# Attention with its value tiles loaded from DRAM: the loads issued from ScalarE's queue in place of SyncE's

## The chip, the core and the metric

The kernel runs on one core of a Trainium2 chip. A core has five engines with an instruction queue each: TensorE (PE: matrix products and transposes into PSUM; its weight loads, PEld, are listed on their own), VectorE (DVE), ScalarE (ACT), GpSimd (POOL) and SyncE (SP, which only issues DMAs and waits). An instruction in a queue waits for semaphores that other engines' instructions or DMAs raise, and what stands behind it in the same queue waits with it. A DMA can be issued from SP's queue or from ACT's (SPq and ACTq in the profile); its data are moved by 16 DMA engines that all queues share.

The metric is the device time of one execution in microseconds (us), and of several executions the median.

## The reference

One decoder layer on 1024 positions of 1024 channels, all in float32. The normalised input is projected; a quarter of the channels goes through a pooling mixer, three quarters through attention with 12 heads of 64. Every head is evaluated with three patterns (all keys of the last 128, every 4th of the last 512, every 16th of the last 2048), and the three results are merged by their softmax denominators. Then come the output projection and a gated feed-forward block. Cut to what matters here:

```python
q, k, v = ...                                  # (B, S, 12, 64) each, of the projection
q, k = rope(q, pos), rope(k, pos)
for window, dilation in ((128, 1), (512, 4), (2048, 16)):
    o, lse = dilated_branch(q, k, v, window, dilation)   # softmax(q k^T / 8, masked) v
    outs.append(o); lses.append(lse)
w = softmax(stack(lses), axis=0)
attn_out = sum(w[..., None] * stack(outs), axis=0)
mix = concatenate([pool_out, attn_out], axis=-1) @ w_out
x = x + rms_norm(mix)
f = (silu(h @ w_gate) * (h @ w_up)) @ w_down             # h = rms_norm(x)
x = x + rms_norm(f)
```

## The kernel before

**Heads and units.** The 12 heads are worked on in six pairs (`pr.p` from 0 to 5). Each pair has two units: `h` = 0 for the first 512 positions, where one dense score table with counted masks serves all three patterns (`dense`), and `h` = 1 for the last 512, with two tables: side 0 for the near keys, side 1 for the keys of the same class modulo 4 (`scores`). So there are 12 units; those of pairs 0 to 3 follow each other, then come (4, 0), (5, 0), (4, 1), (5, 1).

**The stages of a unit.** PE makes the scores into a bank `ps_s`. VectorE adds the mask and takes the extreme (L761, L827), ACT exponentiates in place (L764, L830). For `h` = 1 the two tables are merged (`others`, L853; `join`, L866 to L883), and the rows are weighted on POOL, VectorE or ACT (`weigh`, L894 to L914). PE transposes the weighted rows into `ps_t` (`turn`), ACT copies the high part of the result into `ptr` (L965), VectorE the remainder (L966), and PE multiplies `ptr` with the values into `ps_o` (`product`). At the end of a head ACT and VectorE take `ps_o` out (L1009, L1010) and make the high and low parts of the mix (L924 to L928), which SP stores (L931). Between these steps PE's program has the next pairs' projections (`ps_pj`), whose weights SP loads (L329, L332) and ACT and POOL or VectorE split into high and low parts (L336, L340), and whose results are rotated by VectorE and POOL with the tables `cosr` and `sinr` (L529 to L534). Every float32 product is made of three products of such high and low parts.

**The values.** They are projected for two pairs at once (`v_rows`, and `rows_first` for the first two pairs), split into high and low parts, and stored by SP in the DRAM tensor `vd`, with the positions as rows (L679, L1079). From there each pair's values come back in four loads of 512 KB: `v_load`, L709. Two of them hold the rows in their natural grouping (`nat` = 0: four blocks of 128 positions), two the rows by class modulo 4 (`nat` = 1), for each half `h`. The first of the four is due at one point of the plan, the other three together at another; the table `vt` has the two points of each pair, counted in units.

**Where they go.** `room` picks the place. Pairs 0 to 4 share four tiles of the pool `att` with one buffer each; for `h` = 0 the tags change places from pair to pair, so that the first load of a pair goes into the tile that the former pair is done with first. A load therefore waits for PE's last product with the former pair's values in that tile, as well as for the landing of the stores in `vd`. Pair 5 puts its two loads of `h` = 0 into the places of the tables `cosr` and `sinr`, which must have been read by the last rotation, and the other two into `vlast`.

**What sets the order.** The points at which every step is written into the program are a plan by hand, in units (`put`, `emit`). PE's instructions keep the program's order (`keep_in_program_order`). The order of the others on VectorE, ACT, POOL and SP is worked out when the program is built: a planner runs the program on a model of the chip's times and takes, on each queue, what is ready and of highest priority; some groups have a raised priority (`high_priority`). A DMA is an item of the queue from which it is issued, and it is planned there. The semaphores are added after that.

In the program before, ACT's queue issues three DMAs at the start and two at the end; all others, the 24 loads of L709 among them, are in SP's queue.

Of the kernel before, what the change touches and what calls it, by code (L numbers as in the profile page):

```python
# [8 lines left out]
F32 = mybir.dt.float32  # L9
# [277 lines left out]
def hybrid_block(ctx: ExitStack, tc: tile.TileContext, xT, w_in, w_v, w_vp, w_pool, w_out, w_gate, w_up, w_down,  # L287
                 g1, g2, g3, g4, pscale, cost, sint, maskA, maskB, maskD, quadA, quadB, lsel, ident, perm, band, out):
    nc = tc.nc
# [85 lines left out]
    def slot(k, shape, dt, name):  # L375

        return xgp.tile(shape, dt, name=name, tag="xk%d" % k)
# [190 lines left out]
    def did(key):  # L568
        seen[key] = seen.get(key, 0) + 1

    def need(key, n):
        assert seen.get(key, 0) >= n, (key, n, seen.get(key, 0))
# [116 lines left out]
    def v_load(pr):  # L689

        pr.v = {}

        def room(nat, h):
            if pr.p < NPAIR - 1:
                return att.tile([P, 4, 2, 2, 64], F32R, name="v%d" % nat, tag="v%d%d" % (nat if h else (nat + pr.p) % 2, h),
                                bufs=1)
            if h == 0:

                return att.tile([P, 4, 2, 2, 64], F32R, name="v%d" % nat, tag=("cosr", "sinr")[nat], bufs=1)
            if "v" not in pr.st:  # L700
                pr.st["v"] = slot(4, [P, 2, 4, 2, 2, 64], F32R, "vlast")
            return pr.st["v"][:, nat]

        def load(*which):
            for nat, h in which:
                need(("vd", pr.p // 2, h), 2)
                src = vd[pr.p // 2, h * 512:h * 512 + 512, pr.p % 2 * 256:pr.p % 2 * 256 + 256]
                pr.v[nat, h] = room(nat, h)
                nc.sync.dma_start(pr.v[nat, h].bitcast(F32).rearrange("p b a n f -> p b (a n f)"),  # L709
                                  src.rearrange("(j r) f -> r j f", j=4) if nat == 0 else  # L710
                                  src.rearrange("(r c) f -> r c f", c=4))
                did(("t", pr.p))
            due["v", pr.p, h] = clock[0] + 4.0
        return [lambda: load((0, 0)), lambda: load((1, 0), (1, 1), (0, 1))]
# [431 lines left out]
    for p in range(NPAIR):  # L1146
        pr = Pair()
# [74 lines left out]
    for p in range(1, 4):  # L1222
        pr = pairs[p]
# [824 lines left out]
```

## Time and profile before

| | us |
|---|---|
| median of 3 runs | 1109.18 |
| lowest and highest of them | 1108.96, 1109.7 |
| the profiled execution | 1111.03 |
| its span, first to last instruction | 1109.2 |

| engine | busy us | share of the span |
|---|---|---|
| PE | 1094.4 | 99% |
| VectorE | 782.9 | 71% |
| ACT | 550.7 | 50% |
| POOL | 529.7 | 48% |

The granted clock of TensorE was 0.997 of the full one on the mean.

All rows are of this one execution; times of day are counted from the start of its span. A row of the timeline has the start, the duration, the engine (with a q for its queue: a DMA issue or a wait), the line, the operation and the tiles, written out of the tile left of the arrow; in brackets stands the idle time of the engine before it and what ended it. A row of waits has who waited, for whom, the total in us, the number of times and the longest. The chain of work that ended last goes back from the last instruction, at each step to what released it. Matrix products overlap, so that a PE that is shown busy may still have lost a tenth of a microsecond here and there.

### The profile page before, as it was taken

To read this page: it belongs to the slowest core of one execution; us is meant where nothing else is said; L and a number is where in the kernel's file an instruction comes from. 1 tells how busy PE (TensorE), PEld (TensorE's weight loads), DVE (VectorE), ACT (ScalarE), POOL (GpSimd) and SP (SyncE) were. 2 spreads that over 40 slices of the span, in tenths; PEclk is the share of its full clock that TensorE was granted. 3 is DMA by queue.
4 is the path that set the end of the run, shared out by engine and by line. 5 is a ranking of instruction groups with operands and counts; after the bars stand their busy time and mean duration, and the time that the engine had idled before them with its cause. 6 is when DMAs were issued, how large, how long until landed. Compare 5 with 4: busy or idle time off the path is not lost.

```text
span 1109.2 us, 16017 instructions
## 1 busy us (share of the span) xinstructions
PE 1094.4 (99%) x5646; PEld 929.6 (84%) x5646; DVE 782.9 (71%) x1356; ACT 550.7 (50%) x985; POOL 529.7 (48%) x425
## 2 busy tenths in 40 slices
PE   9999999999999999999999999999999999999997
PEld 7888899989888888888887888888888888888886
DVE  7967978787978758799777777667566462343674
ACT  7456767676777755866222222233222544343432
POOL 0111617263554021100666777686568896666521
PEclk9999999999999999999999999999999999999998
DMA  8225232424149448654466666543445896656442
GB/s 294 95 75 190 96 134 73 156 72 176 58 154 336 156 144 307 225 218 161 164 225 237 237 237 228 209 170 123 152 179 213 277 353 202 206 180 203 133 152 77
DMA packets 91296, 201.81 MB, mean 182 GB/s; under 512 B 9296, under 2 KB 25168, under 8 KB 89808
## 3 DMA queue, kind: packets, MB, share of 16 engines
q1 hardware_dynamic: 90240, 200.00, 51.4%
q8 instruction: 44, 0.72, 0.3%
q10 hardware_dynamic: 976, 0.79, 0.2%
q14 instruction: 36, 0.29, 0.1%
HBM read 143.87 MB, written 56.89 MB: 181 GB/s over the span
## 4 chain that ended last, share of the span: by engine, by line
PE 88%; DVE 5%; ACT 2%; DMA 2%; POOL 2%; issue 1%; ACTq 0%; DVEq 0%; POOLq 0%
PE ps_pj L292 26%; PE ps_s L292 25%; PE ps_o L292 24%; PE ps_t L292 10%; PE ps_t L295 2%; DMA bd<-sq 1%; POOL whl L340 1%; DMA v<-vd 1%; DVE pp L912 1%; DVE ptr L966 0%; DVE ql L561 0%; ACT ptr L965 0%; DMA wraw<-in_w_in_dram 0%; DVE rsw L529 0%; DVE qh L560 0%
## 5 line engine op out<-in xcount | busy, mean ns | idle before, releaser
L292 PE MATMUL ps_o<-tT,fw 128*128 128x512 f32 x648 | 151.0, 390 | 0.8 <-DVE sq L1665 0.8
L292 PEld LDWEIGHTS ps_o<-tT,fw 128*128 128x128 f32 x648 | 121.3, 188 | 26.9 <-issue 1.6
L292 PE MATMUL ps_pj<-x,whl 128*128 128x512 f32 x480 | 131.5, 399 | 0.2 <-DVE whl L340 0.2
L1482 POOL TENSOR_TENSOR fw<-rw,fw 128x512 fp32r<-128x512 f32 x72 | 100.2, 1415 | 29.8 <-ACT fw L1480 28.4
L292 PEld LDWEIGHTS ps_pj<-x,whl 128*128 128x128 f32 x480 | 86.4, 188 | 14.6 <-DVE whl L340 0.7
L340 POOL TENSOR_TENSOR whl<-wraw,whl 128x512 fp32r<-128x512 f32 x44 | 60.2, 1390 | 66.9 <-ACT whl L336 62.2
L1777 POOL TENSOR_TENSOR op<-rw,op 128x512 fp32r<-128x512 f32 x38 | 62.2, 1636 | 31.8 <-ACT op L1776 31.8
L366 POOL TENSOR_TENSOR nrr<-nrr,half 128x4 f32<-128x4 f32 (+1 forms) x7 | 6.9, 985 | 141.2 <-ACT eps L365 99.0
L292 PE MATMUL ps_s<-b,fw 128*128 128x512 f32 x312 | 72.5, 389 | 0.0
L1482 POOL TENSOR_TENSOR whl<-rw,whl 128x512 fp32r<-128x512 f32 x30 | 47.8, 1615 | 44.8 <-ACT whl L1480 29.3
L292 PEld LDWEIGHTS ps_s<-b,fw 128*128 128x128 f32 x312 | 58.6, 188 | 12.2
L1776 ACT ACTIVATE op<-rw 128x1024 fp32r<-128x1024 f32 x38 | 40.0, 1059 | 56.4 <-PE ps_t L292 26.5
L1480 ACT ACTIVATE fw<-rw 128x1024 fp32r<-128x1024 f32 x45 | 47.5, 1062 | 37.1 <-PE ps_o L292 15.2
L292 PE MATMUL ps_pj<-whl,x 128*128 128x256 f32 (+1 forms) x432 | 64.7, 298 | 0.0
L966 DVE TENSOR_TENSOR ptr<-ps_t,ptr 128x512 fp32r<-128x512 f32 (+1 forms) x84 | 53.0, 647 | 15.6 <-ACT ptr L965 15.1
L965 ACT ACTIVATE ptr<-ps_t 128x512 fp32r<-128x512 f32 (+1 forms) x84 | 45.2, 561 | 34.0 <-PE ps_t L295 24.7
L292 PEld LDWEIGHTS ps_pj<-whl,x 128*128 128x128 f32 x432 | 57.3, 191 | 2.2
L1778 DVE TENSOR_TENSOR op<-rw,op 128x512 fp32r<-128x512 f32 x33 | 28.9, 875 | 40.7 <-ACT op L1776 33.0
L1777 POOL TENSOR_TENSOR fw<-rw,fw 128x512 fp32r<-128x512 f32 x26 | 42.7, 1641 | 22.5 <-ACT fw L1776 21.0
L830 ACT ACTIVATE pp<-pp,sx 128x256 f32<-128x256 f32 x96 | 47.9, 501 | 8.2 <-DVE sx L827 7.7
L292 PE MATMUL ps_o<-ptr,v 128*128 128x128 f32 (+3 forms) x376 | 50.4, 268 | 1.2 <-DVE ptr L966 0.8
L1480 ACT ACTIVATE whl<-rw 128x1024 fp32r<-128x1024 f32 x19 | 20.2, 1063 | 61.2 <-DVE rw L1595 36.9
(337 smaller groups left out, 2804.2 us busy)
## 6 DMA issues: line engine op xcount, KB each, us to landing
rw<-bd SPq DMA_DIRECT2D x77, 256.0 KB, 4.0
rw<-in_w_gate_dram SPq DMA_DIRECT2D x28, 512.0 KB, 4.5
rw<-in_w_up_dram SPq DMA_DIRECT2D x28, 512.0 KB, 5.8
v<-vd SPq DMA_DIRECT2D x22, 512.0 KB, 5.0
rw<-wsd SPq DMA_DIRECT2D x44, 256.0 KB, 3.8
bd<-p SPq DMA_DIRECT2D x39, 256.0 KB, 2.8
rw<-in_w_down_dram SPq DMA_DIRECT2D x33, 256.0 KB, 4.4
wraw<-in_w_out_dram SPq DMA_DIRECT2D x15, 512.0 KB, 5.5
```

Source lines behind the costliest of these rows:

```text
L292: return tc.keep_in_program_order(nc.tensor.matmul(*a, **k))
L295: return tc.keep_in_program_order(nc.tensor.transpose(dst, src, by))
L340: pin(eng.tensor_tensor(dst[:, 1, at:at + w], src[:, at:at + w], dst[:, 0, at:at + w].bitcast(F32), ALU.subtract))
L830: nc.scalar.activation(pt[:, j, lo:], pt[:, j, lo:], AF.Exp, bias=sx[:, 0, side, j, hd, 0:1], scale=-1.0, accum_out=sx[:, 0, side, j, hd, ...
L912: nc.vector.tensor_scalar(pv, pv, un.wv[:, side, j, hd:hd + 1], None, op0=ALU.mult)
L965: nc.scalar.activation(ptr[:, 0, :w], t[:, :w], AF.Copy)
L966: nc.vector.tensor_tensor(ptr[:, 1, :w], t[:, :w], ptr[:, 0, :w].bitcast(F32), ALU.subtract)
L1480: nc.scalar.activation(dst[:, :, 0], src, AF.Copy)
L1482: low[0] = eng.tensor_tensor(dst[:, i, 1], src[:, i], dst[:, i, 0].bitcast(F32), ALU.subtract)
L1776: nc.scalar.activation(w[:, :, 0], raw, AF.Copy)
L1777: nc.gpsimd.tensor_tensor(w[:, 0, 1], raw[:, 0], w[:, 0, 0].bitcast(F32), ALU.subtract)
L1778: (nc.gpsimd if p == "P1" else nc.vector).tensor_tensor(w[:, 1, 1], raw[:, 1], w[:, 1, 0].bitcast(F32), ALU.subtract)
```

## The change

The 24 loads of the values are issued from ACT's queue (`nc.scalar`) and no longer from SP's (`nc.sync`). Their sources, places, sizes, points in the plan and dependencies are the same, and so is everything else in the text of the kernel.

```diff
--- before.py
+++ after.py
@@ -706,7 +706,7 @@
                 need(("vd", pr.p // 2, h), 2)
                 src = vd[pr.p // 2, h * 512:h * 512 + 512, pr.p % 2 * 256:pr.p % 2 * 256 + 256]
                 pr.v[nat, h] = room(nat, h)
-                nc.sync.dma_start(pr.v[nat, h].bitcast(F32).rearrange("p b a n f -> p b (a n f)"),
+                nc.scalar.dma_start(pr.v[nat, h].bitcast(F32).rearrange("p b a n f -> p b (a n f)"),
                                   src.rearrange("(j r) f -> r j f", j=4) if nat == 0 else
                                   src.rearrange("(r c) f -> r c f", c=4))
                 did(("t", pr.p))
```

## The prediction

> **What bounds the kernel now.** I began with the page: its span and its shares of the chain of work that ended last.
>
> ```profile
> span 1109.2 us, 16017 instructions
> ...
> PE 88%; DVE 5%; ACT 2%; DMA 2%; POOL 2%; issue 1%; ACTq 0%; DVEq 0%; POOLq 0%
> ```
>
> TensorE (PE) carries the chain; ScalarE (ACT) carries 2% of it. Next, the busy time by stretch (the stretch, then busy time and count of PE, weight loads, VectorE, ACT and POOL, then clock and DMA share):
>
> ```profile
> 80.00:365.00 285.00, 280.10 (x1817) 252.07 (x1816) 232.29 (x609) 199.74 (x483) 127.48 (x136) 1.00 0.42 143
> 80.00:120.00 40.00, 38.08 (x234) 33.36 (x233) 33.24 (x88) 25.94 (x65) 13.13 (x16) 1.00 0.39 132
> 344.00:352.00 8.00, 8.00 (x45) 6.63 (x45) 7.05 (x21) 7.95 (x24) 2.54 (x2) 1.00 1.02 407
> 475.00:880.00 405.00, 404.20 (x1788) 334.06 (x1787) 290.22 (x349) 135.99 (x175) 247.29 (x178) 1.00 0.55 199
> ```
>
> All moved loads are issued between 80 and 365 us. PE is idle there for 285.00 - 280.10 = 4.9 us, ACT for 285.00 - 199.74 = 85.3 us; but from 344 to 352 ACT has no room at all. After 475 PE is full and none of these loads is left, so the change is decided before. Then, who made PE wait in that stretch (total us, times, longest):
>
> ```profile
> PE ps_s L292 <- DVE sd L761: 1.5, 1, 1.5
> PE ps_s L292 <- DVE ex L853: 1.1, 1, 1.1
> PE ps_o L292 <- DVE ptr L966: 0.8, 2, 0.5
> PE ps_o L292 <- DVE dhl L1112: 0.8, 1, 0.8
> PE ps_o L292 <- DMA v<-vd: 0.3, 1, 0.3
> PE ps_pj L292 <- DVE whl L340: 0.2, 1, 0.2
> ```
>
> Seven waits, 4.7 us. What the change could repair directly is the fifth row and perhaps the sixth: 0.5 us. So there is little to win, and PE is tight enough that a late ACT result costs at once.
>
> **The instructions that move.** The rows of the moved line on SyncE's queue (SPq), with durations min/median/max in ns, and of the page's list of DMA issues:
>
> ```profile
> L709 SPq DMA_DIRECT2D v<-vd x22: 360/524/1427, 91.0 to 353.5; - x22
> L709 SPq EVENT_SEMAPHORE  x15: 17/17/28, 85.3 to 352.9; - x15
> L709 SPq DMA_DIRECT2D vlast<-vd x2: 523/570/618, 354.2 to 354.7; - x2
> ```
>
> ```profile
> v<-vd SPq DMA_DIRECT2D x22, 512.0 KB, 5.0
> ```
>
> 24 loads leave SP: 22 x 0.524 + 2 x 0.570 = 12.7 us of issuing, and 15 x 0.017 = 0.3 us of separate waits. An issue on ACT's own queue costs about as much; the last one of this trace is a pair:
>
> ```profile
> 1105.16 0.94 ACTq L1863 DMA_DIRECT2D out_dram<-y  x2
> ```
>
> 0.47 us each, 24 x 0.47 = 11.3 us. I keep SP's price, because it is of the same transfers.
>
> **Term 1, the issues on ACT.** Bounds: 0 if all fall into ACT's idle 85.3 us, 12.7 us if each delays PE in full. A place where they are free is the last four loads:
>
> ```profile
> 352.91 1.19 SPq L709 DMA_DIRECT2D v<-vd  x2
> 354.15 1.19 SPq L709 DMA_DIRECT2D vlast<-vd  x2
> ```
>
> ```profile
> 355.17 0.60 ACT L1009 ACTIVATE low<-ps_o 64x512 f32<-64x512 f32 x1 [2.78 <-PE ps_o L292]
> ```
>
> ACT is idle for 2.78 us before 355.17, waiting for PE, and the four issues take nearly that time, from 352.91 to 355.34. Where ACT stands on the chain they are not free. The chain between 80 and 120 us:
>
> ```profile
> by line: PE ps_pj L292 20.1%; PE ps_o L292 12.4%; ACT pp L830 7.3%; PE ps_s L292 7.0%; DVE pp L912 5.8%; PE ps_t L292 5.4%; PE ps_t L295 4.0%; DVE rsw L529 3.7%; DVE ql L561 3.6%; issue 3.5%; ACT k L553 2.9%; DVE rco L530 2.8%; DVE ptr L966
> ```
>
> ACT's two groups are 10.2% of 40 us = 4.1 us, against 25.9 us of ACT work in that stretch: 16% of what ACT does is on the path. I take 16% of 12.7 = **+2.0 us**. If the cover (waiting for PE) is gone, as from 344 to 352, a load costs its full 0.5 us.
>
> **Term 2, waits that ACT now holds.** Each load waits until PE has read the buffer's former values, and until the turned copy has landed in DRAM. On SP these waits were:
>
> ```profile
> SPq L709 <- PE ps_o L292: 31.2, 8, 7.7
> ...
> SPq L709 <- DMA vd<-vs: 10.6, 3, 5.6
> ```
>
> Behind such a wait on ACT stand the exponentials (L764, L830), the copies of the transposed scores (L965), the high parts of the weights (L336) and the evacuation L1009; VectorE's L966 and L1010 and POOL's L340 wait for them, and PE for these. What a held wait costs, ACT's trace shows once:
>
> ```profile
> L336 ACTq EVENT_SEMAPHORE  x1: 2162/2162/2162, 134.7 to 134.7; - x1
> ```
>
> ```profile
> 134.92 1.09 ACT L965 ACTIVATE ptr<-ps_t 128x512 fp32r<-128x512 f32 x2
> 136.91 1.06 ACT L336 ACTIVATE whl<-wraw 128x1024 fp32r<-128x1024 f32 x1 [0.90 <-issue]
> ```
>
> The queue stood for 2.16 us from 134.7. ACT still worked off what had been handed to it, up to about 136.0, and then sat idle for 0.90. So 0.90/2.16 = 42% of a held wait reaches the engine. Bounds: 0, if the planner, which now orders ACT with these loads in it, puts each behind the moment its buffer is free; 42% of 31.2 + 10.6 = 17.6 us, if ACT holds SP's waits in full. SP had nothing better to do in much of them, and L1009 waits for the same last products of PE anyway, so I go by the single row: 0.90 us of idle at each of the 8 waits on PE, 7.2 us, of which 16% counts: **+1.2 us**. The Trainium skill ("DMA: Bandwidth & Descriptors", section "Anatomy of one DMA — SWDGE (gpsimd) path") says that a DMA's semaphore wait happens on the sequencer that issues it; this speaks against the change, and the L336 row shows such a held queue. By it alone the waits would be ACT's in full, the 17.6 us above.
>
> **Term 3, the transfers themselves.** Only one load is late today. SP's queue and the chain around it:
>
> ```profile
> 331.22 0.89 SPq L1262 DMA_DIRECT2D m<-mixd  x2
> 334.05 0.33 SPq L931 DMA_DIRECT2D mixd<-mix  x1
> 335.57 0.36 SPq L709 DMA_DIRECT2D v<-vd  x1
> ```
>
> ```profile
> 334.85 0.69 DVE rco L530
> 335.54 0.03 DVE pp L827
> 335.57 6.92 DMA v<-vd
> ```
>
> The load goes into the cosine table's place as soon as the last rotation (L530) has read it, and takes 6.92 us against a median of 5.0, behind three transfers that SP issued in the 4.35 us before. PE waits 0.3 us for it. With a queue of its own it may land sooner; from then on PE would wait for nothing there, so at most 0.3 us is to be had. If ACT reaches it late by a held wait, PE waits 2.2 us more. I take **-0.3 us**. The Trainium skill (the same page, section "Queues, rings and completion order") says that each DMA engine takes turns between the queues that have work, which would shorten this load; its section "Issuing engines are not separate DMA queues" says that a second issuing engine saves issue time only. By the first the term is -0.3, by the second 0. What SP gains by standing free (the weights' L329 and L332 come earlier) is at most the 0.2 us of the sixth row; I take nothing.
>
> **Term 4, another order.** PE's order is fixed in the program; that of ACT, VectorE, POOL and SP is worked out by a planner from a model of time, and with 24 more items on ACT it will come out differently in places. The trace can't show the new order. Bounds by its waits: -4.2 us, if the five waits on VectorE's L761, L853, L966 and L1112 go; +17.6 us, if each of the 12 units of attention gains one wait as long as the longest, 1.47. The mean of the seven waits is 0.67 us; I take two more of them, **+1.3 us**.
>
> **Sum.** 2.0 + 1.2 - 0.3 + 1.3 = +4.2 us. The profiled execution took 1111.03 us, 1.83 above its span of 1109.2; the median of the runs is 1109.18, 1.85 below that execution. So 1115.2 on its scale and **1113.4** as a median.
>
> **The rivals.** (B) *All hidden.* ACT's idle 85.3 us takes the 12.7 us, and the waits are short because the planner places the loads well; for it speaks the stretch at 352.9, against it ACT's 7.95 of 8.00 us. The time is 1109.2 plus what falls into 344 to 352, one or two issues: about 1110.
>
> (C) *Faster, by another order on VectorE.* The place is the longest wait:
>
> ```profile
> 225.89 2.01 DVE L912 TENSOR_SCALAR pp<-pp,wv 128x256 f32<-128x256 f32 x4
> 227.81 1.76 DVE L531 TENSOR_TENSOR rsw<-rsw,sinr 128x512 f32<-128x512 f32 x1
> 229.50 0.68 DVE L761 CUSTOM_DVE_ANT_0 pp<-ps_s,mD 128x512 f32<-128x512 f32 x1
> ```
>
> PE waits 1.47 us for L761, which stands behind four weightings (L912) and a rotation (L531). A planner that sees ACT later may put L761 first. If the five waits on VectorE close, 4.2 us go: 1105.0. It decides from the point at which more is closed than terms 1 and 2 cost, 3.2 us. Against it: nothing of the change is aimed at VectorE.
>
> (D) *ACT held.* The planner's times are off by microseconds, and ACT holds SP's waits: 17.6 us of idle and 12.7 us of issues less those 2.4 (1.19 + 1.19) that are covered at 352.9, in all some 28 us, if PE follows ACT: about 1137. Against it: 85.3 us of idle time. By the rule of the Trainium skill quoted at term 2 ("DMA: Bandwidth & Descriptors", "Anatomy of one DMA — SWDGE (gpsimd) path") this is the case to expect.
>
> **Numbers.** My forecast (A) 0.53, between 1111.5 and 1120; B 0.21; C 0.20; D 0.06. A measurement of this kernel tells 0.2%, 2.2 us, from no change: 1107.0 to 1111.4 counts as the same. A and D are slower, 0.59; B the same, 0.21; C faster, 0.20. The range goes from 1105 to 1120; it leaves out D, the better half of C and A's far end.
>
> **What would show it.** Term 1: ACTq rows for L709, 24 of them at about 0.5 us, and ACT's busy time unchanged between 80 and 365. Term 2: gaps of ACT that end on issue beside these rows, longer ACTq EVENT_SEMAPHORE rows on L709. Term 3: the load into the cosine table's place landing in 5 us or less, its wait on PE gone. Term 4: PE's list of waits in this stretch with other entries, of VectorE above all. I am wrong in the main point if PE's idle time between 80 and 365 shrinks below 4.9 us, or if time is lost after 475 us.

## The result and the profile after

The changed kernel took 1113.52 us in the median of seven executions (1112.81 to 1118.13), the kernel before beside it 1110.08 (1108.96 to 1110.65): a ratio of 1.0038, with a 95% interval of 1.0027 to 1.0049. That is 3.4 us slower by the medians and 4.2 us by the ratio. The ratios of this document leave out one later execution, of 1558.88 us at a mean clock of 0.653, of the kernel with products in the wait. The profiled execution took 1113.52 us. From its page:

```profile
span 1111.7 us, 16008 instructions
...
PE 89%; DVE 4%; ACT 2%; POOL 2%; DMA 1%; issue 1%; ACTq 0%; POOLq 0%
...
v<-vd ACTq DMA_DIRECT2D x22, 512.0 KB, 5.4
```

ACT has the same 2% of the chain as before. The median from issue to landing of the loads has gone up, from 5.0 to 5.4 us. The moved line's own rows (durations min/median/max in ns, then first and last start) and the times to landing:

```profile
L709 ACTq DMA_DIRECT2D v<-vd x22: 366/529/947, 90.4 to 356.0; - x22
L709 ACTq EVENT_SEMAPHORE  x10: 17/17/283, 90.1 to 355.4; - x10
L709 ACTq DMA_DIRECT2D vlast<-vd x2: 532/646/761, 356.7 to 357.3; - x2
...
DMA to landing us min/median/max: 3.3/5.4/12.1
```

The issues cost ACT's queue what they had cost SP's. Next the windows (length, busy time of PE, weight loads, VectorE, ACT, POOL, then the granted clock), the stretch from 80 to 365 us and four quarters of a microsecond:

```profile
80.00:365.00 285.00, 278.21 (x1795) 250.05 (x1795) 230.20 (x601) 198.31 (x477) 126.84 (x135) 0.99 0.41 143
345.00:345.25 0.25, 0.25 (x2) 0.15 (x3) 0.25 (x3) 0.25 (x2) 0.00 (x0) 0.82 1.01 401
345.25:345.50 0.25, 0.25 (x2) 0.16 (x1) 0.25 (x1) 0.14 (x2) 0.00 (x0) 0.50 1.14 455
...
348.25:348.50 0.25, 0.25 (x3) 0.25 (x3) 0.00 (x0) 0.08 (x1) 0.25 (x1) 0.50 1.03 422
348.50:348.75 0.25, 0.25 (x3) 0.23 (x3) 0.00 (x0) 0.00 (x0) 0.25 (x2) 0.86 1.08 434
```

PE is idle for 6.8 us of the 285 (4.9 before); ACT's work is the same, 198.31 against 199.74. And PE's clock stands at a half from 345.2 to 348.6. The waits of PE in that stretch (total, times, longest):

```profile
PE ps_o L292 <- DMA v<-vd: 1.8, 1, 1.8
PE ps_s L292 <- DVE sd L761: 1.5, 1, 1.5
PE ps_s L292 <- DVE ex L853: 1.2, 1, 1.2
PE ps_o L292 <- DVE ptr L966: 0.8, 2, 0.5
PE ps_o L292 <- DVE dhl L1112: 0.8, 1, 0.8
PE ps_pj L292 <- DVE whl L340: 0.2, 1, 0.2
```

The list has the entries of before, and one of them has changed: the load into the cosine table's place, the one that the prediction expected to land sooner, costs 1.8 us instead of 0.3. (L853's wait went from 1.1 to 1.2.) The chain around it:

```profile
335.53 0.69 DVE rco L530
336.22 0.03 DVE pp L827
336.25 8.48 DMA v<-vd
344.74 0.14 issue
344.87 0.94 PE ps_o L292 x2
```

ACT issued it at once, 0.03 us after the rotation had read the table, as SP had. But it was 8.48 us on its way, against 6.92.

To see where time goes, take each product of PE and subtract its start in the kernel before from its start in the other one, both counted from the start of the span. I call this the lag. After the change it is 0.2 us at 93, 0.5 at 120 and 0.6 at 288 us; at the product behind this load it jumps to 2.25, and through the slow clock it rises to 3.8 at 348.6. So in this execution two things, the longer wait and the half clock behind it, some 1.6 us each, make most of the loss, at one load out of 24. (About 1.0 us of the lag goes back at 600 us, as it does for most of the kernels below: there the profiled execution of before lost time of its own. The first 10 us of the program vary by up to 2 us between executions. Steps of the lag between 80 and 365 us are therefore what counts.)

Why is the load longer on its way? It does not start sooner. The DMA queues from 337 to 340 us (packets, MB, share; q1 is SP's, q10 would be ACT's) have one row:

```profile
q1 hardware_dynamic: 226, 0.86, 93.5%
```

By the packets in the trace the load's first one moves 4.59 us after the issue, at 340.84; in the kernel before, on SP, it was 4.54 us. What SP had issued earlier goes ahead of it either way. Then the load takes 3.9 us to landing, against 2.4 before, and this is nearly the whole difference. One microsecond in the middle of it:

```profile
q1 hardware_dynamic: 89, 0.32, 79.2%
q10 hardware_dynamic: 82, 0.08, 24.1%
```

That is from 341 to 342 us. What the DMA engines carry for the two queues is 89 packets against 82, but 0.32 MB against 0.08: SP's packets have up to 4 KB, those of the load 1 KB. The queues get about as many packets each, as if they took turns, so ACT's gets half the turns and a fifth of the bytes. SP's share is a store of the mix (L931, issued at 334.72, landed at 342.0) and this transfer, issued 0.23 us ahead of the load and landed at 343.6:

```profile
336.02 0.34 SPq L332 DMA_DIRECT2D wraw<-in_w_out_dram  x1
```

In the kernel before, both went through SP's one queue, the load first. The Trainium skill ("DMA: Bandwidth & Descriptors", section "Queues, rings and completion order") says that a DMA engine takes turns between queues and changes only at the end of a packet; from the load's first packet on the trace agrees, 82 to 89. In the 4.59 us before it ACT's queue moved no packet of this load while SP's moved 1.5 MB; why is not shown.

### The profile page after: what moved, and what is told of

The parts are those of the page before. It is cut to its first block, busy times and chain, and to the rows that moved or that the text cites. A ratio compares the mean times of both kernels' runs of the same rounds, so it can differ in the third digit from the quotient of the medians.

```text
span 1111.7 us, 16008 instructions
## 1 busy us (share of the span) xinstructions
PE 1096.2 (99%) x5646; PEld 931.9 (84%) x5646; DVE 785.9 (71%) x1356; ACT 551.5 (50%) x985; POOL 530.3 (48%) x425
## 4 chain that ended last, share of the span: by engine, by line
PE 89%; DVE 4%; ACT 2%; POOL 2%; DMA 1%; issue 1%; ACTq 0%; POOLq 0%
PE ps_pj L292 26%; PE ps_s L292 25%; PE ps_o L292 25%; PE ps_t L292 10%; PE ps_t L295 2%; DMA v<-vd 1%; POOL whl L340 1%; DVE pp L912 1%; DVE ptr L966 0%; DVE ql L561 0%; ACT ptr L965 0%; DMA wraw<-in_w_in_dram 0%; DVE rsw L529 0%; DVE qh L560 0%; POOL rco L534 0%
## 5 line engine op out<-in xcount | busy, mean ns | idle before, releaser
L966 DVE TENSOR_TENSOR ptr<-ps_t,ptr 128x512 fp32r<-128x512 f32 (+1 forms) x84 | 53.0, 647 | 15.2 <-ACT ptr L965 14.7
L965 ACT ACTIVATE ptr<-ps_t 128x512 fp32r<-128x512 f32 (+1 forms) x84 | 45.3, 562 | 34.0 <-PE ps_t L295 23.2
L830 ACT ACTIVATE pp<-pp,sx 128x256 f32<-128x256 f32 x96 | 47.9, 501 | 9.5 <-DVE sx L827 8.8
L292 PE MATMUL ps_pj<-b,fw 128*128 128x512 f32 x216 | 50.3, 389 | 0.0
```

What stands on the lines that cost most here:

```text
L292: return tc.keep_in_program_order(nc.tensor.matmul(*a, **k))
L830: nc.scalar.activation(pt[:, j, lo:], pt[:, j, lo:], AF.Exp, bias=sx[:, 0, side, j, hd, 0:1], scale=-1.0, accum_out=sx[:, 0, side, j, hd, ...
L965: nc.scalar.activation(ptr[:, 0, :w], t[:, :w], AF.Copy)
L966: nc.vector.tensor_tensor(ptr[:, 1, :w], t[:, :w], ptr[:, 0, :w].bitcast(F32), ALU.subtract)
```

## The experiments

Two places were to be explained: this load, and what is lost in small pieces elsewhere. Every kernel was timed beside the kernel before on the same chip, where that took 1109.8 us in the median for the first four, 1110.43 for the next four, 1110.02 for the two after these and 1110.12 for the last two. Where only the condition differs, only the new line is shown.

**One load back on SP.**

```diff
+                (nc.sync if (pr.p, nat, h) == (NPAIR - 1, 0, 0) else nc.scalar).dma_start(pr.v[nat, h].bitcast(F32).rearrange("p b a n f -> p b (a n f)"),
```

> Undoes one of the 24: the load into the cosine table's place (pair 5, first half, natural rows) goes back to SP's queue, the other 23 stay on ACT's. Theory (that one load is nearly the whole loss): it lands about 6.9 us after its issue as before and not 8.5, PE's wait for it is 0.3 us and not 1.8, TensorE's clock keeps at 1.00 behind it, and the time falls from 1113.5 to about 1110.6, 0.5 us above the kernel before. Rival (ACT pays for its issues, waits and new order all along attention, terms 1, 2 and 4 of the prediction, 4.5 us): the time stays within 1 us of 1113.5.

Measured: 1112.43 us, ratio 1.0024 (1.0015 to 1.0033). The load took 7.86 us and not the 6.9 expected, and PE's wait on it was:

```profile
PE ps_o L292 <- DMA v<-vd: 1.2, 1, 1.2
```

The clock stayed full. So about a third of the loss goes with this load, and neither the theory (1110.6 us) nor the rival (within 1 us of 1113.5) is met. The load is not as quick as before: now the load into the sine table's place, on ACT's queue 1 us later, takes turns with it (203 packets of SP's queue and 177 of ACT's from 343 to 344). And a wait has grown elsewhere, on L761, from 1.5 to 1.8 us.

**That load alone on ACT**, the other 23 on SP as before:

```diff
+                (nc.scalar if (pr.p, nat, h) == (NPAIR - 1, 0, 0) else nc.sync).dma_start(pr.v[nat, h].bitcast(F32).rearrange("p b a n f -> p b (a n f)"),
```

> Does that one part alone: the kernel before with only the load into the cosine table's place issued from ACT, 23 loads on SP. Theory: the load lands after some 8.5 us, PE waits 1.8 us for it and then runs at half clock for some 3 us, and the time is 3 us above the kernel before, about 1113.1. Rival (ACT's 24 issues cost): one issue in 24 costs 0.2 us, so the kernel before to within 0.5 us.

Measured: 1114.66 us, ratio 1.0042 (1.0029 to 1.0055). Moving this one load costs as much as moving all, and 1.6 us more than was expected. The load took 9.04 us and landed at 345.53, PE's product started at 345.67. The wait stands in the list under another name:

```profile
PE ps_o L292 <- ACT pp L830: 2.4, 1, 2.4
```

ACT's L830 ended at 345.63, so by these times alone either could have released the product. But the product starts 0.14 us after the landing, the same 0.14 as in the chain above, and in the kernel before it started at 342.62, ahead of the same L830, which ended at 344.71: it does not need it. The clock stayed full behind these 2.4 us, against the expectation. That was the fastest of six executions: three took 1112.82 to 1113.55 us at a mean clock of 0.997 to 0.998, three 1115.77 to 1116.71 at 0.993 to 0.995.

**Products in the wait**, all loads on ACT. Eight more products are put ahead of the waiting one; their result is overwritten, so that nothing of what is computed changes:

```diff
-                o[hd] = bank("o")
+                o[hd] = bank("o"); [mm(o[hd], pr.k[:, 0, :P], pr.k[:, 0, :512], start=True, stop=True) for i in range(8) if (pr.p, h, hd) == (5, 0, 0)]
```

> All 24 loads on ACT, and eight idle products of 512 columns (1.8 us in all) in PE's order just before the product that waits for the load into the cosine table's place; their result is overwritten. Theory (the second half of that load's cost is the clock, which falls because PE stood still for 1.8 us): PE's wait shrinks to some 0.1 us, the granted clock stays at 1.00, and 1.5 us come back: about 1112.0. Rival (the slow stretch behind the load has another cause, as full DMA engines or late weights): the clock falls all the same, and the time stays at 1113.5 or rises.

Measured: 1113.76 us, ratio 1.0032 (1.0021 to 1.0043). The load took 8.2 us, the clock stayed full there, and the lag at the load rose by 1.5 us, with nothing behind it. The profiled execution has a span of 1111.0 us against 1111.7, but the median is that of the change, and the 1112.0 us expected did not come. So to fill this gap doesn't bring the time back: the load's wait is still lost, and this kernel too has a gap at L761, of 1.84 us, behind which other executions may lose the clock. That the filling kept the clock up is not shown, since it stayed full in the kernel with that load alone on ACT, without it.

**The weights behind the load.** All loads on ACT; the second tile of the output projection's weights is held on SP until ACT has issued the load, by a one-column write into its tile:

```diff
+    def behind_load():
+        with tc.issue_after(loaded[NPAIR - 1, 0, 0].ins):
+            nc.scalar.activation((mark := wpool.tile([P, 1024], F32, name="wraw", tag="wraw", bufs=2))[:, :1], ones, AF.Copy)
+        return mark
...
-                               raw=big(5, [P, 1024], F32, "b5") if own else None)
+                               raw=big(5, [P, 1024], F32, "b5") if own else mark)
```

> All 24 loads on ACT, and the second tile of the output projection's weights, which SP issued 0.23 us before the load into the cosine table's place, is held on SP until ACT has issued that load (a one-column write of ACT into the weights' buffer stands behind the load). Theory A (the two queues take turns packet by packet, and the weights' 4 KB packets get four times the bytes of the load's 1 KB packets): the order of issue is no help, the load still takes 8 to 8.5 us and the time stays at 1113 to 1113.5. Theory B (what is issued first moves first, whichever queue it is on; SP, freed of its waits, only got ahead of the load): the load takes 7.0 us, and the time is about 1110.6.

Measured: 1114.36 us, ratio 1.0043 (1.0031 to 1.0055). The load went out at 339.25 and took 8.09 us, though SP issued the weights 1.1 us after it. The time is above the 1113 to 1113.5 us expected. The queues from 345 to 346:

```profile
q1 hardware_dynamic: 81, 0.32, 78.6%
q10 hardware_dynamic: 83, 0.08, 23.9%
```

The order of the two issues doesn't decide: what comes later on the other queue takes its turns all the same. In this kernel's profile PE waits 1.4 us for the load (the list again puts it down to L830; the product starts 0.14 us after the landing) with the clock full behind it, and the half clock stands behind the gap at L761, 1.80 us.

**The weights in the same queue**, all loads on ACT, and that tile of weights issued on ACT too, behind the load (`raw_tile`, L332; `behind` is the load):

```diff
-        loads.append(nc.sync.dma_start(r.rearrange("p (k m) -> p k m", m=P), src))
+        with tc.issue_after(behind.ins) if behind is not None else ExitStack():
+            loads.append((nc.sync if behind is None else nc.scalar).dma_start(r.rearrange("p (k m) -> p k m", m=P), src))
```

> As after the change, all 24 loads on ScalarE's queue, and the second tile of the output projection's weights is issued on ScalarE's queue too, behind the cosine table's load, so that SP issues nothing from 334.8 to 340. Theory A (turn-taking): the load lands 6.5 to 7.2 us after its issue though it was issued by ScalarE, TensorE's wait on it is 0.2 to 0.8 us, and the time is 1110.5 to 1111.8. Rival (a load issued by ScalarE is slower whatever else runs, or its issue comes late): landing 8 us or more after the issue and a median of 1113 or more as after the change.

Measured: 1112.49 us, ratio 1.0020 (1.0011 to 1.0029). The chain, then ACT's queue from 342 to 343:

```profile
336.87 6.84 DMA v<-vd
343.70 0.14 issue
343.84 0.70 PE ps_o L292 x2
```

```profile
q10 hardware_dynamic: 367, 0.40, 110.3%
```

Issued by ACT, the load takes 6.84 us, as it took 6.92 from SP, once no other queue runs beside it: its queue moves 367 packets in one microsecond, nine of them the weights' 4 KB, instead of 82. Its first packet moved 4.2 us after the issue, and 2.6 us later it had landed. PE's wait is 0.2 us. This shows that the sharing with SP's queue is the cause and not the issuing engine. The median is 0.7 us above what I expected of it; the third pair, below, is still on ACT here.

**Both loads into the tables' places on SP**, 22 on ACT:

```diff
+                (nc.sync if (pr.p, h) == (NPAIR - 1, 0) else nc.scalar).dma_start(pr.v[nat, h].bitcast(F32).rearrange("p b a n f -> p b (a n f)"),
```

> The 22 loads that land elsewhere stay on ScalarE's queue; the two into the places of the cosine and the sine table go back to SP's. Theory A (the loss is the cosine table's load taking turns, packet by packet, with what SP issues): the load lands some 6.9 us after its issue as in the kernel before, TensorE's wait on it is 0.3 us and no product has a lowered clock at 343 to 350; the rest of the loss, if any, is what ScalarE's 22 issues cost along the attention, 0.2 to 1.2 us, so a median of 1110.2 to 1111.2 beside 1110.0 of the kernel before. Theory B (the issues on ScalarE make the loss, at whichever place): the time stays at 1112.5 or above, and TensorE's lag against the kernel before grows by 2 us or more between 90 and 330.

Measured: 1111.44 us, ratio 1.0013 (1.0005 to 1.0022). Two of PE's waits:

```profile
PE ps_s L292 <- DVE sd L761: 1.8, 1, 1.8
...
PE ps_o L292 <- DMA v<-vd: 0.3, 1, 0.3
```

The load takes 6.99 us and its wait is 0.3 us as in the kernel before. The clock is full behind it, as theory A has it. What is left, 1.0 us in the median, within the 0.2 to 1.2 expected, lies along the attention: the lag rises by 0.4 us at 93, by 0.2 up to 120, by 0.2 at 218 and by 0.4 at 230, where the wait on L761 is now 1.8 us.

**The change once more.**

> The changed kernel itself on this chip. Expected: 1113.0 to 1114.0 median; the cosine table's load lands 8 to 9 us after its issue with a wait of TensorE of 1.2 to 2.4 us. Open is whether the clock falls to a half behind the wait as in its first profile: if it does, the wait itself lowers the clock; if it stays at 1.00, the fall is not tied to this wait alone.

Measured: 1115.43 us, ratio 1.0042 (1.0030 to 1.0055), above what was expected. The load took 8.12 us. The profiled execution is the shortest of its six, 1112.61 us:

```profile
PE ps_s L292 <- DVE sd L761: 1.8, 1, 1.8
PE ps_o L292 <- DMA v<-vd: 1.5, 1, 1.5
```

Two long waits, and the clock was full behind both: the fall is not tied to the wait alone. The single times go with the mean granted clock of their execution: 1112.61 us at 0.999, 1114.40 and 1114.89 at 0.997, 1115.98 and 1116.01 at 0.995, 1116.75 at 0.993. So the waits stand in the shortest execution too, and what the others lose beyond it goes with the clock. This is not so in every kernel: with the weights on ACT behind the load, executions of 1113.77, 1114.23 and 1114.37 us had 0.999, and what they lost is not known.

**A load that starts sooner.** The kernel before, all loads on SP, with the mixed blocks of the first half (L1262) issued behind the load and not ahead of it:

```diff
-            nc.sync.dma_start(m[h][n][:, sl].bitcast(F32).rearrange("p k a t -> p k (a t)"),
+            with tc.issue_after(loaded[NPAIR - 1, 0, 0].ins) if h == 0 else ExitStack():
+                nc.sync.dma_start(m[h][n][:, sl].bitcast(F32).rearrange("p k a t -> p k (a t)"),
```

> The kernel before, all loads on SP, with the loads of the first half's mixed blocks issued after the load into the cosine table's place instead of ahead of it. Theory A (what SP has issued ahead sets when the load's packets start, since the queues' packets are served in the order and turn by turn): fewer bytes stand ahead of the load, it lands 3 to 5 us after its issue, its wait of 0.3 us is gone, and the time is 0 to 0.6 us below the kernel before. Rival: the mixed loads come late for the output projection's products, and TensorE waits there: 1 us or more slower. If the load still lands 6.5 us or more after its issue, what stands ahead on SP is not what delays it.

Measured: 1113.0 us, ratio 1.0022 (1.0013 to 1.0032). The load landed 4.07 us after its issue, and its first packet moved after 1.1 us; in the other thirteen kernels, all with the mixed blocks ahead, that took 4.1 to 4.7 us, whichever queue issued the load. So what stands ahead of it does set its time, also from another queue. But the rival holds for the whole:

```profile
PE ps_pj L292 <- DMA m<-mixd: 1.5, 1, 1.5
```

Some 0.4 us are gained at the load and 1.7 us are lost 1 us later. No kernel of this study is faster than the one before.

**The first pair alone on ACT**, and **all but the first pair** (with the tables' two on SP):

```diff
+                (nc.scalar if pr.p == 0 else nc.sync).dma_start(pr.v[nat, h].bitcast(F32).rearrange("p b a n f -> p b (a n f)"),
...
+                (nc.sync if pr.p == 0 or (pr.p, h) == (NPAIR - 1, 0) else nc.scalar).dma_start(pr.v[nat, h].bitcast(F32).rearrange("p b a n f -> p b (a n f)"),
```

> The kernel before with only the first pair's four loads (90 to 93 us) on ScalarE's queue. Theory C (what the spread loss consists of is mostly these four: the first of them waits for the write of the values and holds ScalarE's next eviction, and VectorE behind it runs late for some 30 us): TensorE's lag against the kernel before rises by 0.3 us at 93 and by 0.3 us at 120, and nowhere else; the median is 0.4 to 0.9 us above the kernel before. Rival (each issue costs a little, all through the attention): no step at 93 and 120 and a time within 0.3 us of before.

> All loads but six on ScalarE's queue: the first pair's four and the two into the tables' places stay on SP's. Theory C: TensorE's lag has no steps at 93 and 120, its wait on the load stays at 0.3 us; what is left are 18 issues at other places, 0 to 0.6 us, and the median is 0 to 0.6 us above the kernel before. Rival: the spread loss stays, 0.8 us or more above the kernel before.

Measured: 1110.88 us, ratio 1.0008 (1.0000 to 1.0017), for the first pair alone; its lag rises by 0.4 us at 93 and by 0.2 up to 120, 0.6 in all as expected, and by no more than 0.1 elsewhere before the tables' loads. ACT's timeline of this kernel:

```profile
91.14 0.39 ACTq L709 DMA_DIRECT2D v<-vd  x1
91.58 0.59 ACT L1111 ACTIVATE dhl<-ps_o 64x512 fp32r<-64x512 f32 x1 [0.69 <-DMA vd<-vs]
91.59 1.84 ACTq L709 DMA_DIRECT2D v<-vd  x3
93.54 0.60 ACT L965 ACTIVATE ptr<-ps_t 128x512 fp32r<-128x512 f32 x1 [1.36 <-DVE dhl L1112]
```

An eviction of ACT stands 0.69 us behind a load that waits for the store of the values, and the copy L965 comes after three more issues. So far theory C. But without these four the time was 1113.45 us, ratio 1.0020 (1.0009 to 1.0032), where at most 0.6 us over the kernel before was expected. The steps at 93 and 120 are gone, PE's wait for the cosine table's load is 0.3 us, and the loss is at L761. The windows of this kernel:

```profile
230.00:231.00 1.00, 0.00 (x0) 0.00 (x0) 1.00 (x2) 0.00 (x0) 1.00 (x2) 1.00 0.00 0
...
234.00:235.00 1.00, 1.00 (x7) 1.00 (x6) 0.45 (x2) 0.82 (x3) 0.81 (x1) 0.50 0.86 344
...
236.00:237.00 1.00, 1.00 (x8) 0.92 (x8) 0.65 (x2) 0.97 (x3) 0.00 (x0) 1.00 0.00 0
```

PE waits 1.81 us, and a stretch at half clock follows, which adds 1.6 us to the lag. C had the smaller half.

**The third pair alone on ACT**, and **all but the third pair** (with the tables' two on SP):

```diff
+                (nc.scalar if pr.p == 2 else nc.sync).dma_start(pr.v[nat, h].bitcast(F32).rearrange("p b a n f -> p b (a n f)"),
...
+                (nc.sync if pr.p == 2 or (pr.p, h) == (NPAIR - 1, 0) else nc.scalar).dma_start(pr.v[nat, h].bitcast(F32).rearrange("p b a n f -> p b (a n f)"),
```

> The kernel before with only the third pair's four loads (192 to 208 us) on ScalarE's queue. Theory D (these loads make ScalarE's work late enough that the shift product's chain is 0.3 us late, and TensorE's wait on L761 grows from 1.5 to 1.8 us, over half of the 3.4 us for which the lowered clock lasts, so that some executions lose another 1.7 us to the half clock): TensorE's wait on L761 is 1.8 us, its lag rises by 0.3 to 0.7 us between 205 and 231, and single times lie between 0.5 and 3 us above the kernel before, with the median 0.7 to 3 above. Rival (the long wait on L761 comes from elsewhere, or varies by itself): the wait stays at 1.5 us and the time within 0.4 us of before.

> All loads but six on ScalarE's queue: the third pair's four and the two into the tables' places stay on SP's. Theory D: TensorE's wait on L761 is 1.5 us again and the clock stays at 1.00 behind it; left are the steps of 0.3 us at 93 and at 120, so a median 0.4 to 1.0 us above the kernel before, with no single time over 1113.5. Rival: the wait on L761 is 1.8 us also without these loads, and the time is 1.0 to 3 us above the kernel before.

Measured: 1113.13 us, ratio 1.0022 (1.0010 to 1.0034), for the third pair alone, with single times from 1110.65 to 1116.74; 1111.07 us, ratio 1.0006 (0.9997 to 1.0015), for all but the third, none over 1112.21. Theory D holds in the second. In the first the wait on L761 grew as it says, but the lag and the longest times went past its figures, and no product between 80 and 365 us had a lowered clock in its profile, so that its clause on the clock was not seen there. The chain of this first kernel:

```profile
202.75 6.00 DMA vd<-vs
208.78 0.53 ACTq L709
209.40 0.50 ACT ptr L965
209.93 0.50 DVE ptr L966
...
218.57 1.10 ACT pp L830 x4
...
219.86 0.72 DVE rsw L529
```

The store of the values (SP, L679) is 6.00 us on its way. ACT's queue holds the load that waits for it, then issues it in 0.53 us, and only then comes the copy L965, on which VectorE's remainder (L966) and the next rows depend. ACT's engine shows the hold:

```profile
206.66 0.19 ACT L830 ACTIVATION_READ_ACCUMULATOR pp<-pp,sx 128x1 f32 x1
208.78 0.53 ACTq L709 DMA_DIRECT2D v<-vd  x1
209.40 0.49 ACT L965 ACTIVATE ptr<-ps_t 128x384 fp32r<-128x384 f32 x1 [2.55 <-PE ps_s L292]
```

2.55 us idle; PE's product, to which the row puts it down, is not what came last. The lag rises by 0.5 us at 209, where PE waits for the remainder (L966) behind that copy, by 0.4 at 213, by 0.2 at 218 and by 0.4 at 230, where PE waits for L761:

```profile
PE ps_s L292 <- DVE sd L761: 1.8, 1, 1.8
```

and in the other kernel, with the third pair back on SP and 18 other loads on ACT:

```profile
PE ps_s L292 <- DVE sd L761: 1.5, 1, 1.5
```

This would also explain why the first profile of the change shows 1.5 us there. Its store landed early:

```profile
202.37 0.38 SPq L679 DMA_DIRECT2D vd<-vs  x1
...
206.80 0.53 ACTq L709 DMA_DIRECT2D v<-vd  x1
```

4.4 us from the store's issue to the load's. In the eight other profiles with the third pair on ACT these were 4.9 to 6.0 us, and the wait on L761 was 1.80 to 1.84 us in each; in the five with these loads on SP, 1.47 to 1.50.

## Why the prediction came out right, and where it was wrong

The forecast was slower, at 1113.4 us; 1113.52 was measured (1115.43 when it was run again), and the range held it. The reasons behind it hold only in part, and that the sum meets the time so well is chance.

**Term 3 is the step that failed.** It said -0.3 us: the load into the cosine table's place would land sooner from a queue of its own. After the change it is on its way 1.6 us longer; alone it makes the time 1.0042 (1.0029 to 1.0055) of before. The rule of taking turns was taken for a gain to the load, since it would no longer stand behind SP's transfers. But it stood behind them all the same: its first packet moved 4.59 us after the issue, against 4.54 before. And what SP has issued next to it no longer stands behind the load: it shares with it, at up to 4 KB a turn against 1 KB, and the load takes 3.9 us from its first packet to landing and not 2.4. The bound, "at most 0.3 us is to be had", was right for the gain. The loss was bounded by a held wait on ACT (2.2 us), which never came: ACT issued the load 0.03 us after its condition.

**Term 2 had the right mechanism and a wrong place.** A wait that ACT now holds does cost: 2.55 us of ACT's idle time in the kernel with the third pair alone, and 1.5 us of lag. But it was not any of the eight waits on PE's products, from which the 1.2 us were worked out. It was the other row, the wait for the landing of the store, with 10.6 us on SP, to which the prediction gave nothing of its own in its +1.2. The work behind it on ACT has no need of that store; the eight waits on PE's products left no new entry in PE's list. Where it is moved alone, this pair is worth 2.4 us by the ratio (1.1 to 3.8). What goes beyond the 1.5 us of lag may be the clock in other executions; its own profile does not show a fall.

**Term 1** (+2.0 us for 24 issues) was too large. With 18 loads on ACT, the third pair and the tables' two left out, the ratio is 1.0006 (0.9997 to 1.0015), 0.7 us. The first pair has 0.6 us of lag, by a wait as much as by issues, so that little is left for the others.

**Term 4** (+1.3 us for two new waits) did not come: PE's list has no new entry after the change. Waits that were there grew.

**Rival C** named the right place, the wait on L761 behind four weightings and a rotation, and the wrong direction: nothing moved ahead of it, and a late ACT makes it longer. **B** is out: it gave about 1110, and the interval of the change begins at 1.0027. **D** is far off: PE's idle time grew by 1.9 us and not by 28.

Of what was to show it: ACT's busy time was unchanged and the 24 rows are there. PE's idle time grew to 6.8 us, and no time was lost after 475 us, as the main point asks. The landing in 5 us or less did not come, it was 8.48.

**Open.** The single parts add up to more (1.0042, 1.0022 and 1.0008 alone) than the change as a whole (1.0038 and 1.0042). The intervals are wide enough for most of this. Whether waits share a loss of the clock between them was not tried. Nor was it shown why 22 loads with the third pair among them (1.0013) come out below 18 (1.0020); their intervals overlap. And no run shows why the load's packets start only some 4.5 us after its issue, with ACT's queue free.

## What to carry to other kernels

A DMA on a second queue is not out of the way of the first: here it started no sooner, and then it shared. Count what the other queue moves while it is under way, in packets, and look at whose packets are larger. Before moving an issue to an engine that computes, list what its DMA waits for; a wait for another DMA's landing is one that the engine doesn't have by itself, and what is left of it when the queue gets there stands before the work behind it. Where PE has a wait of about 1.5 us, a few tenths more can cost more than themselves.

## What the runs showed of the hardware

Behind a gap of PE of 1.8 us the clock stood at a half for 3.4 us (345.2 to 348.6 in the windows above), which lost 1.6 us. In the profiles of this study this came behind three of ten gaps of 1.80 us or more between 80 and 365 us (one of 2.40 stayed without), and behind none of nine from 1.44 to 1.52. What decides can be read from the traces. In each profile all changes of the clock lie on one grid of 3.41 us, at another place in each execution. Between 20 and 1095 us, PE's idle time within one stretch of this grid was 1.80, 1.81 and 1.84 us in the three that a stretch at half clock follows. In all other stretches of the fourteen profiles it was 1.65 us or less, since the grid cut the longer gaps: the one of 2.40 us into 0.95 and 1.45. So it looks as if about half a stretch of idle time is what counts, and where the grid lies in an execution decides whether a gap of 1.8 us loses the clock. At the program's end, behind 1095 us, this limit does not hold: in one execution the clock fell there behind 1.0 us of idle time. The Trainium skill ("TensorE: Matmul & The Clock Gate", Part 1) has a free-running window of 3.4 us, and the length agrees; its advice to keep gaps under about 3 us ("Why this matters for your kernels") is not enough here, where 1.8 us did it.

The queues share by packets and not by bytes: 1 KB packets got 0.08 MB in a microsecond against 0.32 MB of SP's, and about 0.36 MB where their queue ran alone. A queue of its own did not let the load start sooner: 4.59 us from issue to first packet on ACT's queue, 4.54 on SP's.
